# Three-pass matmul products on halves of 16 bits in place of halves of 32-bit "round" floats, in a two-layer hybrid decoder trunk

## The chip, the cores and the metric

The kernel runs on one core of one Trainium2 chip. Its time is that of the device, in microseconds, from one launch. Of several runs the median is given. One more run was taken with the hardware profiler; the profile and every answer of its trace come from that one execution. The engines are TensorE (PE for matmuls, PEld for the loading of their weights), VectorE (DVE), ScalarE (ACT), GpSimd (POOL) and SyncE (SP), which issues all DMAs here.

## The reference

Two layers act on x, 512 positions by 1024 channels, float32. Cut to what matters:

```
for l in range(DEPTH):
    h = x @ w_in[l]                                  # 1024 x 9344, all branches read it
    y_rwkv = rwkv7(...)      # 8 heads x 64, a recurrence over the positions
    y_mla  = latent_attention(...)   # rms-normed latents @ w_uq, @ w_ukv, 8 causal heads
    y_conv = conformer(...)  # GLU, depthwise convolution of width 31, LayerNorm
    y_mem  = cross_attention(...)    # 4 heads into 256 memory tokens, mem @ w_mem_kv
    proj   = einsum('bsnc,ncd->bsnd', [each y * silu(gate)], w_o_branch[l])
    merged = sum(sigmoid(merge + b_gate[l]) * proj, axis=branch)
    x = layer_norm(alpha * x + merged @ w_out[l])
```

All of it is float32, and the result must be close to float32. A single 16-bit matmul would not be, so each large product is made in three passes: both operands are split into a high part and what is left of it, and high by low, high by high and low by high are added up in PSUM.

## The kernel before, in words

**Layout.** Most tiles hold channels on the 128 partitions and the 512 positions along the free axis. x is kept as eight pairs of halves (`xh`, `xl`, [128, 512] each, 4 bytes an element). A block of weights is 128 by 1024 floats, 512 KB, in the pool's tag `wr` (two buffers, `WR`). `weights()` issues its DMA and, when it has landed, splits it in two steps, part by part of 512 columns: ACT casts the part to the type float32r (`wh`), DVE subtracts that from the original (`wl`). Six such half blocks can be alive (`WH`). A block of `w_ch` (the input projection, by output channels) holds eight slices of 128 rows by 128 columns.

**Products.** `mm3()` issues the three passes. `project()` makes one block of 128 output channels from eight slices of the contraction: 24 matmuls with 512 columns of x into one bank of PSUM. `merge_items()` does the same with the gated branch outputs `y` and the blocks of `w_o` (its PSUM tile is named po); `wide()`, `narrow()` and `last_item()` with the merged activations `mg` and `w_out` (pz); `lat_item()` with 336 columns of weights that move past x (pl); `memory_items()` with 256 columns (ps_mk, pmv); `latent_items()` and `pair_item()` with the latents `lt` (pqe, pv, pq, pk). Matmuls on operands of 16 bits are there already: the scores and the outputs of both attentions (ms, mo, xs, xo) are three-pass products on float16 halves.

**The recurrence.** Each layer has 16 units (`rwkv_unit`), chains of some 15 small matmul groups of 64x64 (g, gk, p, nv, va, gb, w, yb), with evictions on ACT and DVE between them and a forward substitution on POOL. The causal convolution is 30 fused multiply-adds on DVE for each of four channel blocks (`taps`, tile cacc).

**The order of the work.** While the program is being recorded, `Plan` keeps a clock for every engine and adds each instruction's cost by formulas (those for matmuls are in `MM`). `plan.run()` holds a stream of large items (`project` and so on) and a list of small tasks (attention blocks, recurrence steps, evictions). When the clock of PE reaches the time at which a task's inputs are due, the task is let in between two groups of matmuls. Tasks of the kind "small" wait until `GATHER` or `EDGE` ns of large work have gone by, so that the 64x64 groups come together. Weights are prefetched up to `LOOK` half blocks ahead; a new load is issued when `wlive["raw"]` is under `WR`. So the costs in `MM` and the sizes of the pools decide the order of instructions on every engine.

**The spare.** `Plan.shape()` holds that the first large product after a change of tile shape is dearer when its weights are 32 bits wide. For it, `narrow_low()` makes a float16 copy of the first 128 columns of a block's low part, scaled by 1024 (tile ws, on ACT), and `project()` puts the product of that copy with a scaled float16 copy of x (xs) first in a run, in place of the ordinary low product.

**The end.** `out_after()` adds the last product to the residual (DVE), `norm()` normalizes, `store()` issues the DMA.

Of the kernel before, what the change touches and what calls it, by code (L numbers as in the profile page):

```python
# [35 lines left out]
WR = 2  # L36
WH = 6
WS = 3
SPARE = 1024.0
PROB = 16384.0  # L40
HEADS = 2
RECENT = 12000.0
# [15 lines left out]
PCOL = {}  # L58
# [291 lines left out]
def build(ctx: ExitStack, tc: tile.TileContext, A, out, log, slots, dbg=None):  # L350
# [4 lines left out]
    def MM(o, lhsT, rhs, start, stop, four=False):  # L355
# [40 lines left out]
    wp = pool(WH, name="wp")  # L396
# [82 lines left out]
    def params(l):  # L479
# [6 lines left out]
        V.tensor_scalar(out=h, in0=h, scalar1=0.5, scalar2=None, op0=ALU.mult)  # L486
        g = PCOL["cln_g"]
# [3 lines left out]
        V.tensor_scalar(out=om[:, 0:13], in0=prm[:, 0:13], scalar1=-1.0, scalar2=1.0, op0=ALU.mult, op1=ALU.add)  # L491
# [41 lines left out]
    def halves(name, t, src):  # L533

        h = u(f"{name}h{t}", 512, F32R)
        S.copy(h, src)
        yield
        lo = u(f"{name}l{t}", 512, F32R)
        V.tensor_tensor(out=lo, in0=src, in1=h.bitcast(F32), op=ALU.subtract)
        return h, lo  # L540

    wlive = {"raw": 0, "hl": 0}
    both = set()

    def weights(name, src, parts, last=False, spare=False):
# [8 lines left out]
        def run():  # L554
            e = 0
            for i, (w, c) in enumerate(zip(ws, parts)):
                if last:
                    h, lo = (u(f"{name}{n}{i}", 512, F32R) for n in "hl")
                else:
                    while wlive["hl"] == WH:  # L560
                        yield lambda: wlive["hl"] < WH
                    wlive["hl"] += 1
                    h = wp.tile([128, 512], F32R, tag="wh", name=f"{name}h{i}")[:, 0:c]
                    lo = wp.tile([128, 512], F32R, tag="wl", name=f"{name}l{i}")[:, 0:c]
                yield from split(h, lo, raw[:, e:e + c])
                e += c
                w.extend((h, lo))
                if spare:
                    both.add(lo.tensor.name)
                yield  # L570
            wlive["raw"] -= 1
# [19 lines left out]
    spares = {}  # L591

    def narrow_low(w):

        if len(w) == 2 and w[1].tensor.name in both and plan.now() - plan.tiled < RECENT:
            both.remove(w[1].tensor.name)
            s = wp.tile([128, 128], F16, tag="ws", name="ws" + w[1].tensor.name, bufs=WS)
            S.activation(s, w[1].bitcast(F32)[:, 0:128], AF.Copy, scale=SPARE)
            spares[w[1].tensor.name] = s

    def project(get, xs, name, cols=512):
# [3 lines left out]
        spare, first = None, True  # L605
        for k in range(8):
            if k % 4 == 0:
                h, lo = yield from get()
                spare = spares.pop(lo.tensor.name, None)
# [5 lines left out]
            if spare is not None:  # L615
                if plan.cut != (128, 128) and plan.when(spare) <= plan.now():
                    ops.insert(0, (spare, xs[k - k % 4][2]))
                    spare = None
                elif k % 4 == 3:
                    ops.append((lo[:, 0:128], xs[k - 3][0]))  # L620
                    spare = None
# [65 lines left out]
    def memory_items(l):  # L687
# [4 lines left out]
        def load(pool):  # L692
# [4 lines left out]
            hl = [[pool(f"mem{n}{i}_{l}") for n in "hl"] for i in range(4)]  # L697
# [10 lines left out]
        def keep(x, i, b, ps):  # L708
            return split(*(res[x][i][:, 512 * n + 256 * b:512 * n + 256 * b + 256] for n in range(2)), ps)
# [38 lines left out]
    def half_copy(l, k, src):  # L748

        if k % 4:  # L750
            return ()
        x = xp.tile([128, 512], F16, tag="xs", name=f"xs{k}_{l}", bufs=2)
        S.activation(x, src, AF.Copy, scale=1.0 / SPARE)
        return (x,)

    def layer_items(l):
# [17 lines left out]
        def ch_item(i, name, after, ready=None, picked=None, soon=None):  # L774
# [5 lines left out]
            item([(A["w_ch"][l, i], (512, 512), False, True)], run, ready, picked, soon)  # L780
# [8 lines left out]
        def begin(get):  # L789
            if l == 0:  # L790
# [13 lines left out]
                def splits():  # L804
                    for k in range(8):
                        plan.due(x0[k])
                        yield
                        h = xp.tile([128, 512], F32R, tag="xh", name=f"xh{k}_0")
                        lo = xp.tile([128, 512], F32R, tag="xl", name=f"xl{k}_0")
                        yield from split(h, lo, x0[k])  # L810
                        X[0].append([h, lo])
                    for k in (0, 4):
                        yield
                        X[0][k].extend(half_copy(0, k, x0[k]))

                plan.spawn(splits())
                def later():
# [4 lines left out]
                    yield from load(lambda n: u(n, 512, F32R))  # L822
# [1351 lines left out]
```

## Time and profile before

| what | value |
|---|---|
| median of 3 runs | 1481.43 us |
| lowest and highest run | 1479.6 and 1481.53 us |
| profiled execution: its own time | 1481.95 us |
| profiled execution: span from the first to the last instruction | 1480.1 us |
| mean granted TensorE clock | 0.996 |
| PE busy | 1456.1 us, 98% |
| DVE busy | 1092.2 us, 74% |
| ACT busy | 722.4 us, 49% |
| POOL busy | 236.2 us, 16% |
| mean rate of all DMAs | 109 GB/s |

A group of instructions in the profile has its line, engine, operation, the tiles that it writes and reads (out<-in), the shape, a count, its busy time, the mean of one, and the idle time of the engine before it with what ended that. Lines are mostly those of helpers (L372 is the matmul in `MM`, L287 the call in `Engine`), so groups are told apart by tile. Matmuls overlap: the duration of one (0.39 us for 512 columns) is longer than the step from its start to the start of the next, and it is the step that counts. In the type column float32r products are shown as f32.

### The profile page before, as it was taken

What the parts mean: (1) busy time and instruction counts of PE and PEld (TensorE: products, weight loads), DVE (VectorE), ACT (ScalarE), POOL (GpSimd) and SP (SyncE); (2) the same over time, 40 slices, a digit from 0 to 9 for tenths busy, and PEclk for the clock granted to TensorE, in tenths of its full rate; (3) what the DMA queues carried; (4) which work ended last, traced back from release to release, by engine and by line L of the source; (5) the groups of instructions that cost most, each with busy time, mean ns of one, the idle gap of its engine ahead of it and who ended that gap; (6) DMA issues with size and microseconds to landing.
All of it is one profiled execution on the core that took longest, in us unless ns stands there. A gap on an engine that the chain in (4) does not pass through costs nothing. (4 is left out here: it accounts for less than half of the span.)

```text
span 1480.1 us, 30749 instructions
## 1 busy us (share of the span) xinstructions
PE 1456.1 (98%) x12134; PEld 1191.6 (81%) x12134; DVE 1092.2 (74%) x2418; ACT 722.4 (49%) x1677; POOL 236.2 (16%) x557
## 2 busy tenths in 40 slices
PE   9999999999999999999999998999999999999997
PEld 9986778888888888787998876688888888888886
DVE  6788887898797764544654888888887878556747
ACT  6657675544453543443365556645545444433330
POOL 0000000553064030000010000003630343200000
PEclk9999999999999999999999999999999999999999
DMA  6345574222122223323443355542222122225231
GB/s 225 125 141 115 139 156 130 86 85 91 56 95 63 87 76 101 128 99 118 142 137 113 96 122 134 141 143 85 76 84 88 63 81 85 76 101 183 101 115 72
DMA packets 126545, 161.09 MB, mean 109 GB/s; under 512 B 83776, under 2 KB 85312, under 8 KB 126400
## 3 DMA queue, kind: packets, MB, share of 16 engines
q1 hardware_dynamic: 126400, 159.12, 35.9%
q8 instruction: 95, 1.56, 0.4%
q14 instruction: 50, 0.41, 0.1%
HBM read 133.39 MB, written 5.24 MB: 94 GB/s over the span
## 5 line engine op out<-in xcount | busy, mean ns | idle before, releaser
L287 DVE SCALAR_TENSOR_TENSOR cacc<-hpad,prm,cacc 128x512 f32<-128x512 f32 x240 | 180.5, 752 | 2.4
L287 ACT ACTIVATE tm<-ps_m,prm 128x512 f32<-128x512 f32 x64 | 44.1, 689 | 157.2 <-PE ps_m L372 152.7
L287 POOL TENSOR_SCALAR ZT<-W 32x256 f32<-32x256 f32 x16 | 13.3, 831 | 562.6 <-DMA W<-scr 562.6
L287 POOL TENSOR_TENSOR tmpW<-ZT,W 32x14 f32<-32x14 f32 (+6 forms) x224 | 94.6, 422 | 15.6
L287 DVE SCALAR_TENSOR_TENSOR mt<-tm,po 128x512 f32<-128x512 f32 x48 | 32.9, 685 | 79.1 <-PE po L372 72.1
L287 POOL TENSOR_TENSOR ZT<-ZT,tmpW 32x14 f32<-32x14 f32 (+6 forms) x224 | 85.6, 382 | 17.6
L287 POOL TENSOR_SCALAR gr<-gm 128x4 f32<-128x4 f32 x16 | 5.5, 344 | 261.9 <-DVE gm L287 261.9
L372 PE MATMUL ms<-kT,qT 96*128 96x128 f16 (+3 forms) x192 | 36.6, 305 | 3.8 <-DVE mP L287 3.3
L287 ACT ACTIVATE ms<-ms,nmm 128x128 f32<-128x128 f32 (+3 forms) x64 | 31.9, 499 | 14.4 <-DVE nmm L287 14.2
L287 ACT ACTIVATE mP<-ms,smm 128x128 f16<-128x128 f32 (+3 forms) x64 | 33.1, 527 | 5.8 <-ACT ms L287 3.7
L287 DVE TENSOR_TENSOR merged<-merged,mt 128x512 f32<-128x512 f32 x48 | 33.9, 706 | 1.7
L287 DVE SCALAR_TENSOR_TENSOR mP<-ms,smm,mP 128x128 f16<-128x128 f32 (+3 forms) x64 | 34.2, 544 | 0.2 <-ACT mP L287 0.2
L287 ACT COPY Y<-gb 64x256 f32<-64x256 f32 x32 | 11.7, 367 | 44.0 <-DVE B L287 37.1
L287 DVE TENSOR_REDUCE nmm<-ms 128x1 f32<-128x128 f32 (+3 forms) x64 | 30.0, 481 | 1.1 <-PE ms L372 0.8
L372 PEld LDWEIGHTS <-qT 96*128 96x128 f16 x192 | 13.7, 99 | 20.2 <-issue 13.0
L287 POOL TENSOR_TENSOR lrs<-lrs,mhalf 128x1 f32<-128x1 f32 x8 | 6.2, 773 | 123.8 <-DVE lrs L287 123.5
L287 POOL TENSOR_SCALAR lrs<-lmv 128x1 f32<-128x1 f32 x4 | 1.3, 333 | 139.0 <-DVE lmv L287 133.9
L287 ACT CAST rbh<-w 128x256 fp32r<-128x256 f32 x16 | 6.5, 406 | 33.3 <-DVE w L287 33.3
L287 ACT COPY VA<-va 128x512 f32<-128x512 f32 x16 | 9.4, 586 | 25.1 <-PE va L372 22.8
L287 ACT ACTIVATE xs<-xs,nmx 128x256 f32<-128x256 f32 x32 | 14.4, 449 | 11.6 <-DVE nmx L287 11.6
L287 ACT COPY PP<-p 128x640 f32<-128x640 f32 x16 | 11.1, 694 | 18.1 <-PE p L372 17.9
L372 PEld LDWEIGHTS <-v 128*64 128x64 f16 x480 | 14.1, 110 | 6.6 <-issue 6.0
(3707 smaller groups left out, 5358.8 us busy)
## 6 DMA issues: line engine op xcount, KB each, us to landing
w<-in_w_ch_dram SPq DMA_DIRECT2D x146, 512.0 KB, 3.6
w<-in_w_o_dram SPq DMA_DIRECT2D x32, 512.0 KB, 3.3
w<-in_w_out_dram SPq DMA_DIRECT2D x16, 512.0 KB, 3.4
w<-in_w_lat_dram SPq DMA_DIRECT2D x16, 336.0 KB, 3.4
w<-in_w_mk_dram SPq DMA_DIRECT2D x8, 512.0 KB, 3.7
w<-in_w_mv_dram SPq DMA_DIRECT2D x8, 512.0 KB, 3.3
w<-in_w_qk_dram SPq DMA_DIRECT2D x8, 320.0 KB, 3.1
x<-in_xT_dram SPq DMA_DIRECT2D x8, 256.0 KB, 5.2
```

The lines of the kernel that those rows point to most:

```text
L287: return self.plan.keep(f(*a, **k))
L372: plan.keep(nc.tensor.matmul(o, lhsT, rhs, start=start, stop=stop))
```

## The change

Every operand of a three-pass product becomes a float16 pair: x, the memory tokens, the latents, the gated branch outputs, the merged activations, the low-rank matrices of the recurrence, and the weights. float16 has a narrow range of exponents, so weights are multiplied by 32 (`WSCALE`) before they are split. Each eviction of a product takes the factor 1/32 back, in a scale that it mostly had already, in the parameters of the token shift and the convolution, or in the branch outputs and merged activations when these are split. The matrices `bones` of the recurrence's bonus stay float32r.

- `split()` gets a scale: ACT writes scale times the source as float16, DVE writes scale times the source minus that (one fused instruction).
- `weights()` splits a block whole, 1024 columns in one ACT and one DVE instruction, but for the program's first block and the last item's blocks. Four split blocks can be alive where three could (`WH`), and three raw ones where two could (`WR`).
- `halves()` keeps a pair in one tile of 1024 float16, where it took two tiles.
- The spare (`narrow_low`, `half_copy`, `spares`, `RECENT`, `SPARE`) goes; `project()` calls `mm3()` for every slice.
- The costs of float16 matmuls in `MM` change, and with them the planned order.

The core of the diff; the evictions that only get a factor 1/`WSCALE` are shown by three of them:

```diff
-WR = 2
-WH = 6
-WS = 3
-SPARE = 1024.0
+WR = 3
+WH = 8
+WSCALE = 32.0
...
         if lhsT.dtype == F16 and m <= 64:
-            c = 0.21 * n + 10.0
+            c = 0.2083 * n + 0.9
...
         elif rhs.dtype != F32 or n < 16:
-            c = max(0.4167 * n + 13.0, 66.0 if lhsT.dtype == F16 else 109.0) * (2 if rhs.dtype == F32 else 1)
+            c = 0.4167 * n + 2.2 if lhsT.dtype == F16 else max(0.4167 * n + 13.0, 109.0) * (2 if rhs.dtype == F32 else 1)
...
-    wp = pool(WH, name="wp")
+    wp = pool(WH // 2, name="wp")
...
+        h = prm[:, PCOL["conv_w"]:]
+        V.tensor_scalar(out=h, in0=h, scalar1=1.0 / WSCALE, scalar2=None, op0=ALU.mult)
...
+        V.tensor_scalar(out=prm[:, 0:13], in0=prm[:, 0:13], scalar1=1.0 / WSCALE, scalar2=None, op0=ALU.mult)
...
-    def split(dst_h, dst_l, src):
-
-        S.copy(dst_h, src)
+    def split(dst_h, dst_l, src, scale=1.0):
+
+        if scale == 1.0:
+            S.copy(dst_h, src)
+        else:
+            S.activation(dst_h, src, AF.Copy, scale=scale)
         yield
-        V.tensor_tensor(out=dst_l, in0=src, in1=dst_h if dst_h.dtype == F16 else dst_h.bitcast(F32), op=ALU.subtract)
...
+        if scale == 1.0:
+            V.tensor_tensor(out=dst_l, in0=src, in1=dst_h, op=ALU.subtract)
+        else:
+            V.scalar_tensor_tensor(out=dst_l, in0=src, scalar=scale, in1=dst_h, op0=ALU.mult, op1=ALU.subtract)
+
+    def two(t):
+        return t[:, 0:512], t[:, 512:1024]
+
+    def halves(name, src):
+
+        x = two(u(name, 1024, F16))
+        yield from split(*x, src, 1.0 / WSCALE)
+        return x
...
-            e = 0
-            for i, (w, c) in enumerate(zip(ws, parts)):
+            e, n = 0, len(parts)
+            step = 1 if whole[0] or last else n
+            whole[0] = 0
+            for a in range(0, n, step):
+                c = sum(parts[a:a + step])
                 if last:
-                    h, lo = (u(f"{name}{n}{i}", 512, F32R) for n in "hl")
+                    h, lo = two(u(f"{name}{a}", 1024, F16))
                 else:
-                    while wlive["hl"] == WH:
-                        yield lambda: wlive["hl"] < WH
-                    wlive["hl"] += 1
-                    h = wp.tile([128, 512], F32R, tag="wh", name=f"{name}h{i}")[:, 0:c]
-                    lo = wp.tile([128, 512], F32R, tag="wl", name=f"{name}l{i}")[:, 0:c]
-                yield from split(h, lo, raw[:, e:e + c])
+                    while wlive["hl"] + step > WH:
+                        yield lambda: wlive["hl"] + step <= WH
+                    wlive["hl"] += step
+                    h, lo = (wp.tile([128, 1024], F16, tag="w" + x, name=f"{name}{x}{a}") for x in "hl")
+                h, lo = h[:, 0:c], lo[:, 0:c]
+                yield from split(h, lo, raw[:, e:e + c], WSCALE)
...
-            ops = [(h[:, c], xs[k][1]), (h[:, c], xs[k][0])]
-            if k % 4 or spare is None:
-                ops.append((lo[:, c], xs[k][0]))
...
-            for n, (a, b) in enumerate(ops):
-                MM(ps, a, b, start=first, stop=k == 7 and n == len(ops) - 1)
-                first = False
+            mm3(ps, h[:, c], lo[:, c], *xs[k], k == 0, k == 7)
...
-                        h = xp.tile([128, 512], F32R, tag="xh", name=f"xh{k}_0")
-                        lo = xp.tile([128, 512], F32R, tag="xl", name=f"xl{k}_0")
+                        h = xp.tile([128, 512], F16, tag="xh", name=f"xh{k}_0")
+                        lo = xp.tile([128, 512], F16, tag="xl", name=f"xl{k}_0")
...
-                S.activation(d["t"], ps, AF.Tanh, scale=0.5)
+                S.activation(d["t"], ps, AF.Tanh, scale=0.5 / WSCALE)
...
-                        S.copy(latq[tb][:, 0:336], ps[tb])
+                        S.activation(latq[tb][:, 0:336], ps[tb], AF.Copy, scale=1.0 / WSCALE)
...
-                    V.tensor_tensor(out=zs, in0=zs, in1=ps[:, c - col:c - col + w], op=ALU.add)
+                    V.scalar_tensor_tensor(out=zs, in0=ps[:, c - col:c - col + w], scalar=1.0 / WSCALE, in1=zs, op0=ALU.mult, op1=ALU.add)
...
-            narrow_low(w)
-            if held:
-                narrow_low(held[0])
```

What this does to the order on PE shows at an entry from the recurrence into a gate's product in layer 0. Before (p and the V, M that it reads belong to the recurrence, ps_m is a merge gate's product, wsw52l and xs are the spare copies):

```order
L372 MATMUL po_0_3923<-yxg3h_3103,w51l_3679 128x512
L372 MATMUL p_0_0_0_3938<-V_3245,M_0_0_3895 64x64 x8
L372 LDWEIGHTS wsw52l_3849_3921
L372 MATMUL ps_m_0_3966<-xs_0_260,wsw52l_3849_3921 128x512
L372 MATMUL ps_m_0_3966<-xl_0_158,w52h_3848 128x512
L372 MATMUL ps_m_0_3966<-xh_0_157,w52h_3848 128x512
L372 MATMUL ps_m_0_3966<-xl_0_170,w52h_3848 128x512
```

And such an entry in the changed kernel (g is the recurrence's):

```order
L370 MATMUL po_0_3436<-yxg_0_2722,w50l_3245 128x512
L370 MATMUL g_0_1_3445<-bt_0_1_3396,AR_0_1_3419 64x64 x8
L370 MATMUL g_0_1_3445<-cst,sq_0_1_3360 64x1 x8
L370 LDWEIGHTS w51h_3319
L370 MATMUL ps_m_0_3488<-xl_0_158,w51h_3319 128x512
L370 LDWEIGHTS w51h_3319
L370 MATMUL ps_m_0_3488<-xh_0_157,w51h_3319 128x512
L370 LDWEIGHTS w51l_3320
L370 MATMUL ps_m_0_3488<-xh_0_157,w51l_3320 128x512
```

The spare product no longer comes first, and each product has a weight load of its own in the program, where a float32r product was one instruction. The number of products is the same: 4800 of 512 columns in both orders, attention included. The two kernels have 111 and 110 entries from the recurrence or the attention's narrow matmuls into wide ones; 60 of those before had a spare.

On DVE, the split of block w52 before, amid the convolution (cacc) and a recurrence unit (U, th, cum, V):

```order
L287 TENSOR_TENSOR U_0_0_3832<-p_0_0_0_3800,cst 128x256
L287 SCALAR_TENSOR_TENSOR cacc_0_2421<-hpad_127,prm_241,cacc_0_2421 128x512
L287 TENSOR_TENSOR w52l_3849<-w_3783,w52h_3848 128x512
L287 TENSOR_SCALAR th_1_0_3854<-th_1_0_3854 128x256
L287 SCALAR_TENSOR_TENSOR cacc_0_2421<-hpad_127,prm_241,cacc_0_2421 128x512
L287 SCALAR_TENSOR_TENSOR cum_1_0_3888<-reset,th_1_0_3854 128x256
L287 TENSOR_TENSOR w52l_3885<-w_3783,w52h_3884 128x512
```

And the split of the block of that number in the changed kernel:

```order
L285 SCALAR_TENSOR_TENSOR cacc_0_2453<-hpad_127,prm_241,cacc_0_2453 128x512 x2
L285 SCALAR_TENSOR_TENSOR merged_0_3452<-tm_0_3425,po_0_3436 128x512
L285 SCALAR_TENSOR_TENSOR w52l_3434<-w_3431,w52h_3433 128x1024
L285 TENSOR_SCALAR s_0_0_1_3475<-g_0_1_3445 128x4
L285 RECIPROCAL rn_0_1_3476<-s_0_0_1_3475 128x4
L285 TENSOR_TENSOR Md_0_1_3480<-g_0_1_3445,lm 128x256
```

Two instructions with a recurrence step and a tap between them have become one, and the recurrence's steps stand behind the whole of it. On ACT the two casts become one instruction of 1024 columns, and the 210 casts of spares go; in the order as printed, where equal neighbours share a row, ACT goes from 1551 to 1101 rows and DVE from 2174 to 1935.

More of the change, by code (lines that the diff above doesn't have):

```diff
@@ L524, in rotary, with weights @@
         angles.append(True)
-    def split(dst_h, dst_l, src):
-        S.copy(dst_h, src)
-        yield
-        V.tensor_tensor(out=dst_l, in0=src, in1=dst_h if dst_h.dtype == F16 else dst_h.bitcast(F32), op=ALU.subtract)
[L533 to L540, printed above, removed]
+    def split(dst_h, dst_l, src, scale=1.0):
[3 more added lines that the diff above has]
+            S.activation(dst_h, src, AF.Copy, scale=scale)
+        yield
+        if scale == 1.0:
[8 more added lines that the diff above has]
+        return x
     wlive = {"raw": 0, "hl": 0}
-    both = set()
-    def weights(name, src, parts, last=False, spare=False):
+    whole = [1]
+    def weights(name, src, parts, last=False):
         wlive["raw"] += 1
@@ L554, in run @@
         def run():
-            e = 0
-            for i, (w, c) in enumerate(zip(ws, parts)):
+            e, n = 0, len(parts)
[3 more added lines that the diff above has]
+                c = sum(parts[a:a + step])
                 if last:
-                    h, lo = (u(f"{name}{n}{i}", 512, F32R) for n in "hl")
+                    h, lo = two(u(f"{name}{a}", 1024, F16))
                 else:
-                    while wlive["hl"] == WH:
-                        yield lambda: wlive["hl"] < WH
-                    wlive["hl"] += 1
-                    h = wp.tile([128, 512], F32R, tag="wh", name=f"{name}h{i}")[:, 0:c]
-                    lo = wp.tile([128, 512], F32R, tag="wl", name=f"{name}l{i}")[:, 0:c]
-                yield from split(h, lo, raw[:, e:e + c])
+                    while wlive["hl"] + step > WH:
[4 more added lines that the diff above has]
+                yield from split(h, lo, raw[:, e:e + c], WSCALE)
                 e += c
-                w.extend((h, lo))
-                if spare:
-                    both.add(lo.tensor.name)
+                f = 0
+                for i in range(a, a + step):
+                    ws[i].extend((h[:, f:f + parts[i]], lo[:, f:f + parts[i]]))
+                    f += parts[i]
                 yield
@@ L589, in part @@
             yield plan.when(*xs[k][1:])
[L591 to L599, printed above, removed]
     def project(get, xs, name, cols=512):
@@ L604, in project @@
         ps = pp.tile([128, cols], F32, tag="pp", name="ps_" + name)
-        spare, first = None, True
         for k in range(8):
@@ L696, in load @@
                 DMA(raws[i], A["memT"][:, 512 * i:512 * i + 512])
-            hl = [[pool(f"mem{n}{i}_{l}") for n in "hl"] for i in range(4)]
+            hl = [two(pool(f"mem{i}_{l}")) for i in range(4)]
             for x in "kv":
@@ L708, in keep @@
         def keep(x, i, b, ps):
-            return split(*(res[x][i][:, 512 * n + 256 * b:512 * n + 256 * b + 256] for n in range(2)), ps)
+            return split(*(res[x][i][:, 512 * n + 256 * b:512 * n + 256 * b + 256] for n in range(2)), ps, 1.0 / WSCALE)
         def keys(h):
@@ L779, in run @@
                 yield
-            item([(A["w_ch"][l, i], (512, 512), False, True)], run, ready, picked, soon)
+            item([(A["w_ch"][l, i], (512, 512))], run, ready, picked, soon)
         picked, adds, early = [0] * 4, [0] * 8, [0]
@@ L821, in later @@
                     yield
-                    yield from load(lambda n: u(n, 512, F32R))
+                    yield from load(lambda n: u(n, 1024, F16))
                 plan.spawn(later(), 10000.0)
@@ L829, in begin_rwkv @@
             L["rp"] = open_phase(f"rp{l}")
-            lh, ll, lx = ([L["rp"].tile([128, 512], F32R, tag=n + x, name=n + x + t_) for x in "wa"] for n in ("lh", "ll", "lx"))
+            lh, ll, lx = ([L["rp"].tile([128, 512], F16, tag=n + x, name=n + x + t_) for x in "wa"] for n in ("lh", "ll", "lx"))
             L["lora"] = list(zip(lh, ll, lx))
@@ L1687, in fin @@
                         yield
-                        res[i] = yield from halves(f"y{name}{i}", t_, y)
+                        res[i] = yield from halves(f"y{name}{i}" + t_, y)
                     plan.spawn(fin())
@@ L1697, in fin @@
         def fin(d):
-            merged[d] = yield from halves(f"mg{d}", t_, merged[d])
+            merged[d] = yield from halves(f"mg{d}" + t_, merged[d])
         T = {}
@@ L1750, in run @@
                             plan.spawn(fin(d))
-                blocks = [(A["w_ch"][l, CH_M + 8 * n + 2 * d2], (512, 512), False, True), (A["w_o"][l, n, d2], (512, 512)), (A["w_ch"][l, CH_M + 8 * n + 2 * d2 + 1], (512, 512), False, True)]
+                blocks = [(A["w_ch"][l, CH_M + 8 * n + 2 * d2], (512, 512)), (A["w_o"][l, n, d2], (512, 512)), (A["w_ch"][l, CH_M + 8 * n + 2 * d2 + 1], (512, 512))]
                 if d2 == 0 and n != 3:
@@ L1966, in end_items @@
                 load, its, there = memory_items(l + 1)
-                E["load"] = load(lambda n: E["ep"].tile([128, 512], F32R, tag=n[:5], name=n))
+                E["load"] = load(lambda n: E["ep"].tile([128, 1024], F16, tag=n[:4], name=n))
                 for n in ORDER:
```

56 lines of the change are left out of this document (19 added, 37 removed).

## The prediction

> **What bounds the kernel now.** I read the profile's summary first, then the busy times by stage, what PE waited for, the chain that ended last, and single stretches of PE's timeline. From the summary, the span, the busy engines and the granted TensorE clock in 40 slices:
>
> ```profile
> span 1480.1 us, 30749 instructions
> PE 1456.1 (98%) x12134; PEld 1191.6 (81%) x12134; DVE 1092.2 (74%) x2418; ACT 722.4 (49%) x1677; POOL 236.2 (16%) x557
> PEclk9999999999999999999999999999999999999999
> ```
>
> PE is never idle for long and runs at full clock. By stage (columns: span, busy PE, PEld, DVE, ACT, POOL, granted clock, DMA share, GB/s):
>
> ```profile
> 100.00:200.00 100.00, 97.90 (x610) 72.18 (x611) 83.45 (x225) 65.56 (x182) 0.00 (x0) 1.00 0.65 145
> 900.00:1000.00 100.00, 94.28 (x580) 71.16 (x579) 87.19 (x188) 58.36 (x145) 0.00 (x0) 0.97 0.56 143
> 1000.00:1100.00 100.00, 100.00 (x1135) 81.59 (x1134) 87.21 (x188) 50.20 (x121) 47.43 (x110) 1.00 0.27 85
> 1300.00:1400.00 100.00, 100.00 (x680) 80.89 (x679) 61.58 (x131) 36.66 (x75) 4.38 (x5) 1.00 0.37 127
> ```
>
> Only the two attention stages, 100 to 200 and 900 to 1000, leave PE idle, 7.8 us together. The largest of PE's waits in the whole span:
>
> ```profile
> PE ms L372 <- DVE mP L287: 3.3, 3, 1.9
> PE ps_val L372 <- ACT w154h L287: 2.0, 1, 2.0
> ```
>
> They are single events. So the time is the number of matmuls by the step from one to the next. Two stretches of products from the chain, one with DVE 87% busy and one in the quiet end (start, length, group):
>
> ```profile
> 1029.29 5.56 PE ps_m L372 x24
> 1362.93 21.76 PE ps_m L372 x96
> ```
>
> A 32-bit product of 512 columns takes 0.232 us beside a busy DVE and 0.2267 in the quiet.
>
> **The products.** The price of a 16-bit one stands in this trace too, in the cross-attention's output:
>
> ```profile
> 143.79 0.59 PE L372 MATMUL xo<-xTh,vm 128*128 128x512 f16 x2
> 144.22 0.38 PE L372 MATMUL xo<-xTl,vm 128*128 128x512 f16 x1
> 144.44 0.38 PE L372 MATMUL xo<-xTh,vm 128*128 128x512 f16 x1
> ...
> 148.89 0.59 PE L372 MATMUL xo<-xTh,vm 128*128 128x512 f16 x2
> 149.32 0.38 PE L372 MATMUL xo<-xTl,vm 128*128 128x512 f16 x1
> 149.53 0.38 PE L372 MATMUL xo<-xTh,vm 128*128 128x512 f16 x1
> ```
>
> Three steps in 0.65 and three in 0.64 us: 0.215, in a stage where DVE is 83% busy. So a product of 512 columns wins 0.0117 us in the quiet (0.2267 - 0.215) and 0.017 beside a busy DVE (0.232 - 0.215). I take 0.013, nearer to the quiet end, because only parts of the other stages have DVE and ACT both at work.
>
> How many there are follows from the weight loads and from what each block feeds:
>
> ```profile
> w<-in_w_ch_dram SPq DMA_DIRECT2D x146, 512.0 KB, 3.6
> w<-in_w_o_dram SPq DMA_DIRECT2D x32, 512.0 KB, 3.3
> w<-in_w_out_dram SPq DMA_DIRECT2D x16, 512.0 KB, 3.4
> w<-in_w_lat_dram SPq DMA_DIRECT2D x16, 336.0 KB, 3.4
> ```
>
> A w_ch or w_o block feeds 8 slices by 3 products: 178 x 24 = 4272. The w_out blocks give 264 of 512 columns (and 240 of 256), the 8 w_qk blocks 15 each (120), the 2 w_v blocks 24 each (48): 4704, of which 60 are 16-bit already (the spare copies). 4644 x 0.013 = 60 us, between 54 and 79. The narrower ones, 384 of 336 columns from w_lat and 760 of 256, I price at the quiet difference, as if it were a fixed cost of each product: 1144 x 0.0117 = 13; none has a 16-bit twin of equal form, so from 0 to 20.
>
> The Trainium skill (TensorE: Matmul & The Clock Gate, Back-to-back issue gap) gives about 131 ns as the sustained step of a 512-column product in a real kernel. By that figure the products would win some 450 us, not 60; these rows measure 215.
>
> **Entries.** A run of products begins after the recurrence's 64x64 matmuls, or after a 128-column one. Without and with the spare copy, and after the attention's bf16 mask:
>
> ```profile
> 275.74 0.50 PE L372 MATMUL po<-yxg2l,w48h 128*128 128x512 f32 x1
> 276.07 0.39 PE L372 MATMUL po<-yxg2h,w48h 128*128 128x512 f32 x1
> 276.31 0.40 PE L372 MATMUL po<-yxg2h,w48l 128*128 128x512 f32 x1
> ...
> 289.15 0.39 PE L372 MATMUL ps_m<-xs,wsw50l 128*128 128x512 f16 x1
> 289.61 0.40 PE L372 MATMUL ps_m<-xh,w50h 128*128 128x512 f32 x1
> ...
> 897.31 0.22 PE L372 MATMUL ms<-causal,idb 128*128 128x128 bf16 x1
> 897.65 0.40 PE L372 MATMUL ps_glu<-xh,w151h 128*128 128x512 f32 x1
> ```
>
> The third product starts 0.57 us after the first without the spare and 0.46 with it. The change drops the spare, but now every product is of the spare's kind, so I expect 0.43 (two steps) everywhere. By the order of the instructions there are 60 entries with a spare, which save 0.03 (2 us), and 17 without, which save about 0.14 (2 us). The 47 entries after the bf16 mask take 0.34 to the second product, against 0.28 for a quarter step and a 32-bit step; 0.06 each, 3 us. Sum 7, I count 6; from 0 to 8.
>
> **The halves of weights and activations.** A block's halves were made by two ACT casts and two DVE subtractions; now by one of each on the whole block. The old pieces, and the 16-bit forms of two widths:
>
> ```profile
> L287 ACT CAST w52h<-w x2: 618/620/623, 289.9 to 291.5; 128x512 fp32r<-128x512 f32 x2
> L287 DVE TENSOR_TENSOR w52l<-w,w52h x2: 712/732/751, 291.0 to 293.5; 128x512 fp32r<-128x512 f32 x2
> ...
> L287 DVE SCALAR_TENSOR_TENSOR xP<-xs,smx,xP 128x256 f16<-128x256 f32 x32 | 15.2, 476 | 0.0
> L287 DVE SCALAR_TENSOR_TENSOR mP<-ms,smm,mP 128x512 f16<-128x512 f32 x16 | 11.9, 744 | 0.2 <-ACT mP L287 0.2
> ```
>
> 476 to 744 ns for 256 more columns gives 1.28 us at 1024, against 2 x 0.73: some 212 x 0.18 = 38 us less of DVE. At the worst it is two of 744, nothing gained. ACT has about 2 x 0.62 against one of some 1.1, and the 210 spare casts go. None of this is on PE's path, since DVE is 74% and ACT 49% busy; its cover is the prefetch, now three raw blocks and four split ones instead of two and three. If that cover failed, each block would expose up to 1.1 + 1.28 us. What is queued behind the longer DVE instruction waits 0.55 us more: the reductions of the attention and the masks of the recurrence, for which PE has other products to run. The scales of 1/32 ride on evictions that exist already; out_after's add becomes a fused one on the same operands; only the last stands on the path, at the very end, for at most 0.1 us. Four small DVE instructions on parameters run while PE has products. No DMA is added, but a third raw block lets one more 512 KB load (3.6 us to landing) stand in SP's queue ahead of the attention's transposes; its price is part of the next term.
>
> **What is given back.** In the two attention stages DVE chains, not PE, sometimes end last. 5% off about 190 us of PE there is 10; DVE's relief pays for half. I count 5 us lost, from a gain of 5 (the relief wins) to 18 (the whole 10 and the idling doubled).
>
> **Sum.** 60 + 13 + 6 - 5 = 74 off the profiled run. Its own time, 1481.95, is 1.9 more than its span of 1480.1 and 0.5 more than the median of the runs, 1481.43. What lies around the span does not change, so the median becomes 1481.4 - 74 = 1407.
>
> **The rivals.**
>
> *PE waits for late halves or DVE chains in more places (0.08).* A gap costs more than itself. The place with the largest one, and its two windows (PE's busy time first, the clock after POOL):
>
> ```profile
> 927.70 0.80 PE L372 MATMUL ps_val<-xl,w154h 128*128 128x512 f32 x1 [1.98 <-ACT w154h L287]
> 928.29 0.63 PE L372 MATMUL ps_val<-xh,w154h 128*128 128x512 f32 x1
> 928.72 0.63 PE L372 MATMUL ps_val<-xl,w154h 128*128 128x512 f32 x1
> ...
> 925.00:930.00 5.00, 3.02 (x13) 2.08 (x10) 4.93 (x13) 3.87 (x12) 0.00 (x0) 0.67 0.35 93
> 930.00:935.00 5.00, 5.00 (x17) 3.26 (x15) 4.75 (x14) 3.90 (x11) 0.00 (x0) 0.64 0.28 57
> ```
>
> After 1.98 us of idling, the products step at 0.43 and the granted clock is 0.67, then 0.64: the place costs 2 us of waiting and about 2 of half speed, 4. Six to fifteen such places more give 1430 to 1470. The Trainium skill (the same page, The HAM clock gate) ties half speed to an idle window of about 3.4 us; by that rule a gap of 2 us would cost only itself. The trace decides for 4.
>
> *The same, on the other side: slower (0.04).* Place: the recurrence, where a 1.28 us split can stand ahead of a unit's small DVE steps. One gap of 4 us in each of the 16 units gives back 64 of the 74; it turns slower from the 19th place. Against it: 1000 to 1100 has PE at 100.00 with DVE at 87%.
>
> *A 16-bit product steps no faster in a long run (0.03).* Each is now two instructions to fetch, weights and product, and the longest 512-column 16-bit run here has six. Then at most the 6 us of the entries come: 1475. Against it: the six run at 0.215 throughout.
>
> *More than I count (0.05).* The busy difference holds for nearly all products (79 instead of 60) and the attention stages' 7.8 us of idling go, with the 5 us given back: 1407 - 19 - 8 - 5 = 1375, so 1375 to 1393. Of this 0.05, less than 0.01 is for 16-bit products that step faster in long runs than in runs of six. With the skill's 131 ns that would be about 950 us.
>
> **The numbers.** The forecast has 0.80: 1407, from 1393 (0.016 for each 512-column product, 14 more) to 1428 (the quiet difference, 6 less; 18 lost to waits in place of 5, 13; entries, 2). That is also the range for 8 in 10, since the rivals outside hold 0.20. Under 0.2%, about 3 us, a measurement of this kernel can tell nothing from no change. Faster has 0.95, the same 0.01, slower 0.04.
>
> **What would show it.** In the changed kernel's trace, products of 512 columns step at 0.215 to 0.218 in the quiet end and beside busy DVE alike; the third product after the recurrence starts 0.43 us after the first; weight splits on DVE last 1.2 to 1.3 us; PE's waits stay under some 20 us in all; the clock stays at 1.00 outside the attention stages. The forecast is wrong if the products step at 0.227, if PE's busy share falls under 95% between 200 and 600, or if the waits of PE name split weights again and again.

## The result, and the profile after

The changed kernel takes 1457.4 us (median of 4 runs, 1456.1 to 1457.7), the kernel before 1480.5 us on the same chip (1479.2 to 1481.5). The ratio is 0.984, with a 95% interval from 0.983 to 0.986. It is faster, as forecast, but by 23 us and not by 74: 1457 lies outside the range of 1393 to 1428. The profiled run took 1457.4 us itself, with a span of 1455.6.

The summary of the changed kernel's profile:

```profile
span 1455.6 us, 29966 instructions
PE 1396.6 (96%) x12134; PEld 754.1 (52%) x12134; DVE 1069.8 (73%) x2186; ACT 650.3 (45%) x1227; POOL 242.2 (17%) x557
PEclk9999999999999989999999999999999999999999
```

PE is busy for 60 us less than the 1456.1 of before, but it is idle for 59 us of the span (1455.6 - 1396.6) where it was for 24. One digit of the granted clock has come down to 8, in the fifteenth slice of 36 us, from 509 on. The stages (span, busy PE, PEld, DVE, ACT, POOL, granted clock, DMA share, GB/s):

```profile
100.00:200.00 100.00, 97.71 (x637) 50.15 (x636) 83.31 (x216) 63.70 (x158) 0.00 (x0) 1.00 0.65 140
400.00:500.00 100.00, 95.44 (x1441) 54.71 (x1430) 83.81 (x200) 39.99 (x83) 46.89 (x114) 1.00 0.16 52
500.00:600.00 100.00, 92.15 (x775) 47.67 (x768) 60.04 (x124) 33.24 (x49) 11.26 (x27) 0.91 0.35 119
900.00:1000.00 100.00, 94.82 (x595) 45.49 (x593) 83.41 (x150) 48.24 (x93) 0.00 (x0) 0.98 0.56 147
1000.00:1100.00 100.00, 99.05 (x1122) 52.23 (x1121) 86.34 (x173) 45.98 (x86) 46.92 (x101) 1.00 0.27 85
1200.00:1300.00 100.00, 95.17 (x1156) 52.30 (x1155) 70.46 (x159) 41.09 (x71) 26.65 (x66) 0.97 0.25 86
1300.00:1400.00 100.00, 95.35 (x615) 44.13 (x614) 54.69 (x101) 31.47 (x44) 2.40 (x4) 0.97 0.34 118
```

Before the change, three of these stages read:

```profile
400.00:500.00 100.00, 100.00 (x1172) 81.69 (x1165) 84.23 (x192) 47.14 (x109) 40.47 (x102) 1.00 0.25 79
500.00:600.00 100.00, 100.00 (x1039) 80.21 (x1038) 59.60 (x144) 40.66 (x94) 14.74 (x36) 1.00 0.26 85
1200.00:1300.00 100.00, 100.00 (x1176) 81.23 (x1175) 70.10 (x170) 48.72 (x113) 31.70 (x79) 1.00 0.27 89
```

The attention stages, 100 to 200 and 900 to 1000, look as they did. New are the idle stretches at the end of each layer's recurrence, 400 to 600 and 1200 to 1400, where PE was never idle before. The products themselves, from the chain that ended last (start, length, group):

```profile
1051.86 5.18 PE ps_mg L370 x24
1379.58 15.54 PE ps_m L370 x72
```

5.18 / 24 and 15.54 / 72 are both 0.216 us, beside a DVE that is 86% busy (1000 to 1100) and in the quiet end alike. What PE waited for, the largest rows:

```profile
PE xo L370 <- DMA xTl<-xP: 6.8, 5, 2.4
PE yb L370 <- ACT Y L285: 3.6, 1, 3.6
PE ty L375 <- DVE yb L285: 3.5, 1, 3.5
PE nv L370 <- DVE NQ L285: 3.1, 2, 2.6
PE w L370 <- DVE cn L285: 2.5, 1, 2.5
```

Split weights are not on top. Four of the five rows are links of the recurrence or of the convolution's normalization (cn). PE's timeline at the worst place (start, length; in brackets the idle time before and what ended it):

```profile
503.07 0.44 PE L375 MATMUL tk<-cst,v 128*128 128x128 f32 x2
504.81 0.41 PE L375 MATMUL tk<-cst,bt 128*128 128x128 f32 x2 [1.30 <-DVE cn L285]
505.06 0.38 PE L375 MATMUL tk<-cst,kt 128*128 128x128 f32 x2
508.09 0.71 PE L370 MATMUL nv<-vt,NQ 64*64 64x64 f32 x16 [2.65 <-DVE NQ L285]
508.73 1.11 PE L375 MATMUL ct<-cst,cacc 128*128 128x128 f32 x4
509.63 0.64 PE L375 MATMUL ty<-cst,yb 128*128 128x128 f32 x2
512.77 0.48 PE L370 MATMUL w<-H,Gs 64*64 64x64 f32 x4 [2.50 <-DVE cn L285]
```

Not one large product stands between the small ones. PE steps along the recurrence and the convolution's transposes (ct), and each gap is bare. Why nothing was ready shows in the convolution's taps. The rows of its last taps (shortest, median, longest in ns, first and last start), of before and then of the changed kernel:

```profile
L287 DVE SCALAR_TENSOR_TENSOR cacc<-hpad,prm,cacc x5: 737/747/1123, 430.1 to 442.8; 128x512 f32<-128x512 f32 x5
```

```profile
L285 DVE SCALAR_TENSOR_TENSOR cacc<-hpad,prm,cacc x4: 745/752/768, 482.2 to 499.5; 128x512 f32<-128x512 f32 x4
```

The first layer's last tap starts at 499.5 instead of 442.8, although the work on PE takes less time. The planner lets in the convolution's gates and its share of the merge, the large products meant for the end of the recurrence, only when the convolution's result is there. The first product of those gates (ps_cg) starts at 529.0, after the dry spell; before the change it started at 492.9, while the recurrence still had some 120 us to go. With nothing set between its steps, the recurrence itself was over sooner: its last transposes (ty) stand at 558 instead of 612.

In the second layer the last tap is not later by the clock: it ends at 1170.0, before the change at 1179.3. But PE has no large product left from 1200 on and idles from 1204, and the gates start at 1212.2 (before, at 1230.5). Whether the taps are the cause there too is for the experiments to show.

The reason lies in a rule of the planner. A tap is a task marked "slack": it falls due only when the planner's clock of DVE is not ahead of that of PE. It takes the time that DVE has to spare beside PE. With products 5% shorter, PE's clock comes to the same point of the work sooner, DVE's own work there is hardly less, and so less of DVE is spare.

### The profile page after: what moved, and what is told of

The parts are those of the page before. It is cut to its first block, busy times and chain, and to the rows that moved or that the text cites. A ratio compares the mean times of both kernels' runs of the same rounds, so it can differ in the third digit from the quotient of the medians.

```text
span 1455.6 us, 29966 instructions
## 1 busy us (share of the span) xinstructions
PE 1396.6 (96%) x12134; PEld 754.1 (52%) x12134; DVE 1069.8 (73%) x2186; ACT 650.3 (45%) x1227; POOL 242.2 (17%) x557
## 5 line engine op out<-in xcount | busy, mean ns | idle before, releaser
L285 POOL TENSOR_TENSOR ZT<-ZT,tmpW 32x14 f32<-32x14 f32 (+6 forms) x224 | 92.8, 414 | 17.6
L370 PEld LDWEIGHTS <-mg 128*128 128x128 f16 x504 | 49.3, 98 | 34.0
L285 ACT ACTIVATE mP<-ms,smm 128x128 f16<-128x128 f32 (+3 forms) x64 | 33.0, 527 | 13.5 <-issue 8.5
L370 PEld LDWEIGHTS <-xh 128*128 128x128 f16 x256 | 25.0, 98 | 13.8 <-issue 2.5
L370 PEld LDWEIGHTS <-qT 96*128 96x128 f16 x192 | 17.1, 98 | 17.1 <-issue 3.5
L285 DVE SCALAR_TENSOR_TENSOR z<-pz,z 128x256 f32<-128x256 f32 (+1 forms) x15 | 7.7, 512 | 20.9 <-PE pz L370 20.9
L285 ACT ACTIVATE mg<-merged 128x512 f16<-128x512 f32 x16 | 10.1, 630 | 28.1 <-DVE merged L285 28.1
L285 DVE SCALAR_TENSOR_TENSOR merged<-tm,po 128x512 f32<-128x512 f32 x16 | 11.0, 686 | 14.2 <-PE po L370 9.3
```

The costliest lines, as they stand in the source:

```text
L285: return self.plan.keep(f(*a, **k))
L370: plan.keep(nc.tensor.matmul(o, lhsT, rhs, start=start, stop=stop))
```

## The experiments

Two theories stood against each other. The first: the loss comes from those late taps. The second: it comes from splitting whole blocks, with instructions of 1.05 us on ACT and 1.23 us on DVE. A third question was how much of the price is the half clock that follows a gap.

**1. Taps a little earlier.** The planner's rule, in `Plan.run()`:

```diff
                 elif task[2] == "slack":
-                    task[0] = max(task[0], self.clk["DVE"])
+                    task[0] = max(task[0], self.clk["DVE"] - 400.0)
```

> The changed kernel with one rule of its planner altered: a convolution tap is recorded as soon as DVE is planned at most 0.4 us ahead of PE, and no longer only when DVE is not ahead at all. Instructions and their number are the same. Theory 1 (the products did get faster, but the convolution, whose taps only fill DVE's spare time, now comes too late, so PE runs out of ready products around 485 to 523 us and later, waits, and falls to half clock): 1430 to 1444, that is 13 to 27 us under the changed kernel's 1457, and the stretch of half clock at 506 gone. Theory 2 (the splits of whole blocks, 1.05 us on ACT and 1.23 on DVE, make weights and chains late): 1453 to 1461, as the change.

Measured: 1443.8 us (1442.3 to 1445.1), 0.975 of the kernel before (0.973 to 0.977), 14 less than the change as it is. The last taps of the first layer and the two stages:

```profile
L285 DVE SCALAR_TENSOR_TENSOR cacc<-hpad,prm,cacc x5: 741/743/752, 376.6 to 384.2; 128x512 f32<-128x512 f32 x5
```

```profile
400.00:500.00 100.00, 100.00 (x1240) 55.23 (x1238) 77.01 (x174) 47.30 (x89) 40.69 (x96) 1.00 0.24 73
500.00:600.00 100.00, 100.00 (x1158) 52.12 (x1156) 59.59 (x135) 34.71 (x56) 17.34 (x38) 1.00 0.32 103
900.00:1000.00 100.00, 92.45 (x572) 43.71 (x570) 84.29 (x156) 49.51 (x97) 0.00 (x0) 0.95 0.52 133
1200.00:1300.00 100.00, 100.00 (x1267) 54.15 (x1260) 66.63 (x162) 40.49 (x72) 29.86 (x68) 1.00 0.29 94
```

The dry spells are gone, 100.00 from 400 to 600 and from 1200 to 1300, with the same instructions. The first theory holds for these places. But the gain is at the low end of what it foretold: the attention stage, 900 to 1000, has become worse (92.45 for 94.82), and so has the stage ahead of it, 800 to 900 (88.54 for 94.06).

**2. The same rule in the kernel before** (200.0 in place of 400.0; half the lead).

> The kernel before the change with the same rule (0.2 us here). Theory 1: no dry spell is there to remove, PE is 98% busy, so 1477 to 1484, no difference from 1480.5. If the rule is simply better whatever the products cost, 1455 to 1470.

Measured: 1495.4 us (1492.3 to 1497.4), 1.010 of before (1.008 to 1.011): neither. It costs 14 us. The two attention stages of this run:

```profile
100.00:200.00 100.00, 92.68 (x567) 67.44 (x566) 81.60 (x211) 60.57 (x165) 0.00 (x0) 0.97 0.59 133
900.00:1000.00 100.00, 92.10 (x610) 68.32 (x610) 86.07 (x195) 59.48 (x151) 0.00 (x0) 0.95 0.60 143
```

In the kernel before, PE was busy for 97.90 and 94.28 us of them. With no dry spell to close, the new order mainly worsens the attention stages: of the 10.5 us that PE idles more, 7.4 lie there. So the rule is not simply better; it pays where the taps are what comes last.

**3. Halves again, with the taps' rule of the first experiment.** In `weights()` and its pool (pieces of at most 512 columns, eight buffers of 512):

```diff
-    wp = pool(WH // 2, name="wp")
+    wp = pool(WH, name="wp")
...
-            step = 1 if whole[0] or last else n
+            step = 1
...
-                    h, lo = (wp.tile([128, 1024], F16, tag="w" + x, name=f"{name}{x}{a}") for x in "hl")
+                    h, lo = (wp.tile([128, 512], F16, tag="w" + x, name=f"{name}{x}{a}") for x in "hl")
```

> The first experiment (0.4 us rule) with every block split in pieces of at most 512 columns again, as before the change: some 420 casts and 420 subtractions instead of 209 of each. Theory 2: over 5 us faster than the first experiment, because each half comes 0.5 us sooner. Theory 1: within 6 us of the first experiment, PE's waits named after split weights no fewer.

Measured: 1422.3 us (1421.1 to 1423.7), 0.960 of before (0.959 to 0.962), 21.5 less than the first experiment, although DVE and ACT have more to do. This is the second theory's outcome; the reason given with it, that each half comes sooner, is put to the test in the twelfth. The summary's line:

```profile
PE 1386.5 (98%) x12134; PEld 747.8 (53%) x12134; DVE 1080.6 (76%) x2422; ACT 673.7 (47%) x1463; POOL 234.5 (17%) x557
```

DVE is 16 us busier than in the first experiment (1064.4), and PE idles 32.8 us of 1419.3 instead of 50.6 of 1441.4.

**4. Keeping PE warm.** The changed kernel's order; where the planner lets PE wait for over 0.5 us, products with zero weights are issued into the bank that is being filled (they add zero) or into a free one:

```diff
                     last = 0.0
+                    if self.fill is not None and min(times) > now + 500.0:
+                        self.fill(now, min(times))
                     self.clk["PE"] = max(now, min(times))
...
+    def fill(now, until):
...
+        for _ in range(int((until - now - 60.0) / 216.0)):
+            plan.keep(nc.tensor.matmul(o, zw, zx, start=first, stop=end))
```

> The changed kernel in its own order, with 97 products of 512 columns with zero weights (they add zero, or go to a spare bank) set into the waits of PE that the order foresees, 21 us in all, most of them between 484 and 515. They do no work: they only keep PE from idling. If half clock after idling is a cost of its own (41 us at half clock cost some 17 to 20 more than the waits): 1441 to 1450. If waiting itself is all the cost: 1456 to 1460.

Measured: 1449.4 us (1448.5 to 1451.0), 8 less than without the zeros: idling has a price beyond itself. The dry spell in the changed kernel, and the same 20 us here (busy PE first, granted clock after POOL):

```profile
500.00:520.00 20.00, 12.27 (x284) 10.00 (x276) 13.38 (x38) 4.27 (x9) 7.10 (x22) 0.66 0.26 85
```

```profile
500.00:520.00 20.00, 18.31 (x260) 10.84 (x251) 13.32 (x38) 4.76 (x10) 6.40 (x21) 1.00 0.33 110
```

0.66 has become 1.00. In the whole run, PE's busy time at half clock goes from 32 to 10 us.

**5. Halves alone,** the edit of the third experiment without the taps' rule.

> The changed kernel with blocks split in pieces of at most 512 columns again and nothing else altered (the taps' rule as in the change). If the split of whole blocks costs some 21 us by itself, as between the first and the third experiment, and adds to the late taps: 1432 to 1442. If the 21 us hung on the order that the first experiment happened to get: anything from 1447 up, with the taps ending as late as in the changed kernel or later.

Measured: 1500.1 us (1499.7 to 1500.6), 1.013 of before: slower than the kernel before, and 43 us slower than whole blocks. This is what was expected if the 21 us hung on the first experiment's order: the two costs do not add. With halves DVE has more to do (1089.9 us), so it has even less to spare: the first layer's last tap ends at 514.8, the second's at 1252.8, where the changed kernel had 500.2 and 1170.0.

```profile
500.00:600.00 100.00, 81.41 (x738) 43.62 (x734) 59.95 (x139) 31.44 (x59) 18.13 (x40) 0.88 0.30 101
1200.00:1300.00 100.00, 81.97 (x1237) 51.96 (x1236) 73.80 (x198) 33.85 (x77) 31.46 (x88) 0.85 0.14 42
```

The dry spells are more than twice as deep, at the same two places (18.6 us idle for 7.9, and 18.0 for 4.8). Here the first theory is shown from the other side: taps later, spells deeper.

**6 and 7. A second pair,** whole blocks and halves with the taps' lead at 600.0.

> Whole blocks, the taps' rule at 0.6 us in place of 0.4: another order of the same instructions. Theory 1 (late taps): 1436 to 1450, about as the first experiment's 1443.8.

> The same rule of 0.6 us with blocks split in halves. If the split of whole blocks is a cost of its own: 14 to 26 us under the kernel with whole blocks and 0.6 us. If the third experiment won by the luck of its order: within 8 us of it.

Measured: 1454.3 us (1453.0 to 1458.1) with whole blocks, 1429.6 (1426.3 to 1430.5) with halves: 24.8 between them. The order differs from the first pair, the difference hardly. The whole blocks' 1454 lies above what was expected of it: in the stage from 800 to 900 PE is busy for 82.21 us, where the first experiment had 88.54. An earlier tap is not always a gain. PE's lines:

```profile
PE 1391.0 (96%) x12134; PEld 750.1 (52%) x12134; DVE 1063.7 (73%) x2186; ACT 652.7 (45%) x1227; POOL 236.3 (16%) x557
```

```profile
PE 1381.8 (97%) x12134; PEld 747.2 (52%) x12134; DVE 1080.2 (76%) x2422; ACT 675.1 (47%) x1463; POOL 239.0 (17%) x557
```

Of 1451.2 and 1424.5 us of span, 60 and 43 are idle.

**8. Halves and three numbers of the planner altered** (`EARLYN` 1 for 3, `EARLY` 5 for 4, `GATHER` 5000 for 6500, lead 400.0).

> Halves and the rule of 0.4 us, with three of the planner's other numbers altered as well (small work gathered for 5 us instead of 6.5, the branch whose gates may come early another one, five of them instead of four). If the order alone sets what is left: 1408 to 1424; PE idle 15 to 25 us and half clock under 15 us in all. No theory has it under 1400, since PE's own work stays at some 1385 us.

Measured: 1419.9 us (1416.4 to 1423.7), 0.958 of before (0.956 to 0.960). It beats both kernels, but its runs overlap those of the third experiment: the three numbers change nothing that can be told. PE idles 36 us, more than the 15 to 25 expected.

**9 to 12. Which property of the whole-block split?** All four start from the first experiment (whole blocks, lead 400.0, 1443.8). The ninth cuts only the subtraction on DVE in two, the tenth only the cast on ACT, each with room for other work between the pieces:

```diff
-                yield from split(h, lo, raw[:, e:e + c], WSCALE)
+                S.activation(h, raw[:, e:e + c], AF.Copy, scale=WSCALE)
+                for p in range(0, c, 512):
+                    q = slice(p, min(p + 512, c))
+                    yield
+                    V.scalar_tensor_tensor(out=lo[:, q], in0=raw[:, e:e + c][:, q], scalar=WSCALE, in1=h[:, q], op0=ALU.mult, op1=ALU.subtract)
```

> Whole blocks with the taps' rule of 0.4 us (the first experiment, 1443.8), where only the subtraction on DVE is cut in two pieces of 512 columns, with room for other DVE work between them; the cast on ACT stays whole, and both halves are still handed over together. If what costs is the 1.23 us instruction that the chains of attention and recurrence find ahead of them on DVE: most of the 21 us comes, 1422 to 1431. If it is that the halves of a block come late together: 1438 to 1448.

> The same with the parts exchanged: the cast on ACT is cut in two pieces, the subtraction on DVE stays whole at 1.23 us. If DVE's long instruction costs: 1438 to 1448. If ACT's long one (1.05 us, ahead of exponentials and evictions) costs: 1422 to 1434.

The eleventh gives more room (`WH` 12 for 8). The twelfth issues both instructions as two pieces directly one behind the other, so that PE's order is exactly that of the first experiment:

> The first experiment with room for six split blocks instead of four, its order of instructions else unaltered. If the whole blocks cost by holding up the split of the next one until a whole block's room is free: 1424 to 1436. If the length of the instructions costs, not the room: 1440 to 1447, as the first experiment.

> The first experiment in exactly its order on PE, where each whole cast and each whole subtraction is issued as two pieces of 512 columns directly one behind the other, with nothing let in between; PE waits for each piece by itself. ACT and DVE are occupied as long as before or some 0.1 us longer a piece, but the first half of a block is ready about 0.6 us sooner. If a block's first half comes too late: 1424 to 1436 against the first experiment's 1443.8. If it is what must queue behind the long instruction, or the order that is planned around it: 1442 to 1449.

Measured: 1435.2 (1434.4 to 1436.5) with DVE's part cut, 1434.1 (1433.4 to 1435.0) with ACT's, 1443.8 (1442.4 to 1450.2) with more room, 1440.9 (1438.5 to 1443.0) with the pieces in place. Cutting either long instruction brings 9 to 10 of the 21.5 us. Both lie between what the two readings expected (the tenth at the edge of one): neither instruction is the whole of it. Room is worth nothing. That a block's first half is ready earlier is worth some 3 us at most, since the runs of the twelfth overlap those of the first. PE's waits by name agree. In the first experiment they are 41.3 us in all, of which 13.5 name split weights; in the third 23.2 and 6.7. So most of what halves save is waits for other things. In the twelfth the waits for split weights fall to 8.6, but all waits together stay at 41.0.

**All kernels in one account.** Idle is the span less PE's busy time; "half" is half of the time in which PE was busy at a granted clock of 0.5, counted in the trace; the rest is what PE would take without either.

| kernel | span | idle | half | rest |
|---|---|---|---|---|
| before | 1480.1 | 24.0 | 2.9 | 1453 |
| before, taps' lead 0.2 (2) | 1495.6 | 34.5 | 9.0 | 1452 |
| changed | 1455.6 | 59.0 | 16.2 | 1380 |
| lead 0.4 (1) | 1441.4 | 50.6 | 13.3 | 1377 |
| lead 0.4, halves (3) | 1419.3 | 32.8 | 6.5 | 1380 |
| halves alone (5) | 1497.9 | 84.5 | 30.7 | 1383 |
| lead 0.6 (6) | 1451.2 | 60.2 | 10.1 | 1381 |
| lead 0.6, halves (7) | 1424.5 | 42.7 | 5.4 | 1376 |
| halves, tuned (8) | 1421.9 | 36.4 | 4.9 | 1381 |
| DVE's part cut (9) | 1433.7 | 46.4 | 7.4 | 1380 |
| ACT's part cut (10) | 1432.0 | 46.8 | 8.8 | 1376 |
| more room (11) | 1442.2 | 53.1 | 11.2 | 1378 |
| pieces in place (12) | 1441.2 | 50.3 | 11.5 | 1379 |
| zeros in the waits (4) | 1449.2 | 41.2 | 4.8 | 1403, 21 of it zeros |

The rest falls in two groups, 1452 to 1453 with 32-bit halves and 1376 to 1383 with 16-bit ones (the fourth without its zeros, too). The products' own gain is 73 us from the kernel before to the changed one and between 70 and 77 in every kernel that has it; nearly all of the differences between 1420 and 1500 us are idling and half clock.

## Why the prediction was right about the products and wrong about the waits

*The product's step* was right: 0.216 for the forecast 0.215 to 0.218, in the quiet and beside a busy DVE. The Trainium skill (TensorE: Matmul & The Clock Gate, Back-to-back issue gap) has 131 ns as the sustained spacing in a real kernel and says that its formula for a single matmul, some 216 ns, over-counts there; this trace has the 216 in stretches of 72 products, so the rows decided rightly.

*Products and entries.* The terms 60 + 13 + 6 made 79. Measured is the difference of the rests, 1453 - 1380 = 73. The third product of a run starts 0.43 to 0.44 us after the first (medians, after the mask and after 64x64 groups), as forecast.

*The splits.* DVE's instruction of 1024 columns averages 1.23 us, within 1.2 to 1.3. Its busy time fell by 22 us (1092.2 to 1069.8), not by 38. The scale costs nothing: a subtraction of 512 columns averages 0.69 us with it (third experiment) and without it (before). The durations of the weights' subtractions, added up, fell by 41 us, about as forecast. But in both traces neighbouring instructions on DVE overlap, by 0.057 us on average, so 232 fewer of them lose 13 us of overlap, and DVE's other instructions take 7 us more.

*The cover failed.* The prediction costed the splits at nothing, with the prefetch as their cover, and said of what is queued behind the longer instruction that "PE has other products to run". With the taps in time, whole blocks cost 21.5 and 24.8 us against halves in two pairs. The cut of DVE's part and that of ACT's part bring about 9 each, so it lies with the long instructions on both engines, not with the room and hardly with the late first half. It depends on the order, though: with the late taps of the change itself, halves were 43 us slower. What stays open: whether the chains wait behind the long instruction on the chip, or whether the planner, which prices it, makes a worse order around it. An order for halves can't be run with whole blocks, so the two were not told apart.

*The step that failed most: "What is given back".* The prediction read that "Only the two attention stages, 100 to 200 and 900 to 1000, leave PE idle", looked for losses there alone, and counted 5 us (-5 to 18). The reading was wrong already: PE idled 24.0 us before the change, 7.8 of them there and 16 at the start, between 600 and 900 and at the end. What was given back is 48, not 5: idling went up by 35 and half clock by 13. By the spans the change gained 25 in place of 74; 6 of the missing 49 are the products', 43 are these. In those two stages almost nothing changed. Some 22 us of idling are new between 400 and 600 and between 1200 and 1400, the rest lies at the start, at 200 to 300 and at 700 to 900. Rows of 100.00 were read as room, and they were not: they say that PE was last there, not by how much. The taps fill what DVE has to spare beside PE, and the recurrence's end is filled with products that wait for the taps. A shorter PE takes from both.

*The rivals.* "PE waits for late halves or DVE chains in more places" is what happened. It had 0.08. It counted six to fifteen places more at 4 us each, and 1457 is 50 us above the forecast, some twelve of them; in the traces, gaps of 1 us or more before an instruction of PE went from 7 to 18. Its 4 us rested on the gap of 1.98 us that cost as much again in half clock, and the fourth experiment bears that out as a cost of its own. But the place was read too simply: another gap, of 1.89 us, had ended 3 us before, and PE was busy at half clock for 5.9 us around and behind the second, which is 3 us lost.

In the changed kernel the trace has six stretches at half clock before the end, 3.4, 3.4, 17.1, 3.4, 6.8 and 6.8 us long. The first follows two short gaps:

```profile
46.98 0.39 PE L370 MATMUL ps_val<-xl,w11h 128*128 128x512 f16 x1 [1.42 <-ACT w11h L285]
47.20 0.38 PE L370 MATMUL ps_val<-xh,w11h 128*128 128x512 f16 x1
48.67 0.43 PE L370 MATMUL ps_val<-xh,w11l 128*128 128x512 f16 x1 [1.09 <-DVE w11l L285]
48.90 0.63 PE L370 MATMUL ps_val<-xl,w11h 128*128 128x512 f16 x1
49.33 0.63 PE L370 MATMUL ps_val<-xh,w11h 128*128 128x512 f16 x1
```

The Trainium skill (the same page, The HAM clock gate) has a free-running window of some 3.4 us, and half clock after an idle one. The lengths agree, all multiples of 3.4; the need for a whole idle window does not, since gaps of 1.42 and 1.09 us, with two products between them, were enough here. The place of the slower rival, a split ahead of the recurrence's steps, was near to where it happened; its cause was not the split but the taps. (Its 16 units are those of the whole program, 8 in each layer.)

*"More than I count"* did not happen. Its last figure, about 950 us, does not follow from the prediction's own numbers: 450 us for the products in place of 60 in the same sum make 1017.

*The test set by the prediction* caught it: PE's busy share fell under 95% between 500 and 600.

## What to carry to other kernels

A stage where the bound engine is 100% busy has a margin that the profile does not show. Before forecasting that a faster engine will stay busy, find what fills it at the end of each serial chain and which other engine's leftover time makes that filler ready: work that is scheduled "when there is time" can come too late when the bound engine gets faster. And one instruction in place of two saves the issuing engine's time but can cost more than that in waits elsewhere, so measure it apart from the change that it came with. Measure it in the order that will be kept, too: halves of blocks cost 43 us with the late taps and saved 21.5 with the early ones. Here the two edits together gave 23 us, and the type change with the old pieces and taps recorded 0.4 us sooner gave 59.

## What the runs showed of the hardware

A gap of the same size may or may not cost half clock. In the third experiment a gap of 2.0 us is soon followed by products that step at 0.43; in the changed kernel one of 2.2 us is not:

```profile
595.33 0.68 PE L375 MATMUL ty<-cst,yb 128*128 128x128 f32 x2 [2.01 <-DVE yb L285]
...
596.89 0.63 PE L370 MATMUL ps_m<-xh,w99h 128*128 128x512 f16 x1
597.32 0.63 PE L370 MATMUL ps_m<-xh,w99l 128*128 128x512 f16 x1
```

```profile
203.73 0.39 PE L370 MATMUL xo<-xTl,vm 128*128 128x512 f16 x1 [2.21 <-DMA xTl<-xP]
...
204.39 0.38 PE L370 MATMUL xo<-xTl,vm 128*128 128x512 f16 x1
204.60 0.59 PE L370 MATMUL xo<-xTh,vm 128*128 128x512 f16 x2
```

What decides is more than the length of one gap. In each of the 14 traces, all stretches at half clock start and end on one grid of steps of 3.41 us (but for the end of the last, which is that of the program). Four such steps of the changed kernel (length, busy PE, and the granted clock after POOL); the first and the third are followed by half clock, and the fourth is the step behind the third:

```profile
45.47:48.89 3.42, 0.91 (x4) 0.23 (x4) 3.41 (x9) 2.38 (x3) 0.00 (x0) 1.00 0.55 224
202.49:205.90 3.41, 2.17 (x11) 1.09 (x12) 2.14 (x6) 1.83 (x6) 0.00 (x0) 1.00 1.01 222
209.31:212.73 3.42, 1.39 (x9) 0.66 (x7) 3.39 (x9) 1.34 (x4) 0.00 (x0) 1.00 0.41 79
212.73:216.14 3.41, 3.01 (x8) 1.17 (x9) 0.17 (x2) 0.26 (x1) 0.00 (x0) 0.50 1.32 214
```

PE idled 2.51, 1.24 and 2.03 us in the first three. The gap of 2.21 us got by because the edge at 202.49 cut it in two, 0.97 and 1.24; the gap of 2.01 us in the third experiment lay whole in one step, 593.10 to 596.51. Counted over all 14 traces, each of the 48 steps at full clock in which PE idled more than 2.0 us, in one gap or several, was followed by half clock; of those with 1.5 to 2.0 us 16 of 46 were, and of the 5635 with less, one. From half clock, PE came back after every step with under 0.19 us of idling (52) and after none with over 0.8 (34). So a gap of 2 us is priced between 2 and 4 us, not at 4 each. Products with zero weights in the waits kept the clock up and saved 8 us, although PE did no work for as long as before: 41 us idle and 21 of zeros, against 59 idle. A float16 weight load takes far less of PE's loading side than a 32-bit one, 754 us for the same 12134 loads that took 1192, but PE was busy for 98% of the span where that side was for 81%. Whether the longer load is what makes a 32-bit product's step longer, no run here shows.
